# Two dense projections of a decoder block (w_o and w_xq) turned into streamed Strassen products, with the weight sums re-timed

## The chip, the cores and the metric

One core of one Trainium2 chip. The metric is the device time of the whole kernel in microseconds (us); the median of three runs before the change is 1949.75 us (1947.55 to 1952.03). Engines in the text: PE (TensorE, matrix products), DVE (VectorE), ACT (ScalarE), POOL (GpSimd), SP (SyncE, which issues nearly all the transfers between HBM and SBUF). Each engine works through its own queue in order, and so does SP with the transfers it issues.

## The reference, cut to what matters

The block has batch 1, 1024 tokens, width 1024 and one layer, all in float32: two mixers side by side (an SSD scan and a gated linear attention), their gated merge, an output projection `w_o` with a residual add, cross-attention to 256 memory tokens, and a SwiGLU feed-forward of inner width 2816.

```python
def hybrid_mixer(...):
    ...
    merged = jax.nn.sigmoid(g_ssd) * (y_ssd @ w_up_ssd) + jax.nn.sigmoid(g_gla) * (y_gla @ w_up_gla)
    return merged @ w_o

def mem_cross_attention(n, m, w_xq, w_xkv, w_xo):
    q = (n @ w_xq).reshape(Bsz, S, XATTN_HEADS, XATTN_HEAD_DIM)
    ...
    p = jax.nn.softmax(s, axis=-1).astype(v.dtype)
    o = jnp.einsum('bhsm,bmhd->bshd', p, v).reshape(Bsz, S, D_MODEL)
    return o @ w_xo

h = h + hybrid_mixer(rmsnorm(h, norm_mix), w_in, ...)
h = h + mem_cross_attention(rmsnorm(h, norm_xattn), rmsnorm(mem, norm_mem), w_xq, w_xkv, w_xo)
h = h + swiglu(rmsnorm(h, norm_ffn), w_ffn_in, w_ffn_out)
return rmsnorm(h, norm_final)
```

So `w_up_ssd`, `w_up_gla`, `w_o`, `w_xq` and `w_xo` are five products of 1024x1024 by 1024x1024, in this order, with the attention between the fourth and the fifth.

## The kernel before, in words

**Arithmetic.** Activations lie transposed (features on the 128 partitions, tokens along the row, in two halves of 512). A float32 product is made of three products of a shorter float type: each operand is split into a high part (ACT copies it, L227) and a low part (DVE subtracts, `split`, L226 to L228), and PE multiplies high by high, high by low and low by high into one PSUM bank. All matmuls are issued by one helper (L51), all DVE and POOL operations by another (L73), so groups of the trace are told apart by their tiles.

**Stages in order.** Input projection (Strassen), SSD, GLA, the products `w_up_ssd` (called dense 0), `w_up_gla` (1), `w_o` (2), `w_xq` (3), attention, `w_xo` (4), then the feed-forward: gate and up products as Strassen units, and the down product as a streamed Strassen.

**dense (L1236 to L1253)** is the classical product: 8 output blocks of 128 features by 2 halves of tokens, and for each 8 input blocks by 3 products, hence 16 x 24 = 384 matmuls of 128x512. Its weights come through `Left` (L1190 to L1219): one 1 MB load (`raw`, in a slot called "aux") brings 256 columns, and each 128 of them are split into a ring of two tiles `wd` two blocks ahead of their use. One `Left` serves all five products, so that the loads of one run on into the next. `residual` (L1357) adds the old residual to what `w_o` gives, stores the sum (`h1_d`), scales it and splits it into the operand of `w_xq` (`put_xq`), and adds up its squares (`s1`).

**presum (L1297 to L1318)** makes sums and differences of quarters of `w_ffn_out` for the streamed down product and keeps them in `down_d` in HBM. It works in 11 chunks on a single tile `pre`: one 1 MB load, four POOL operations of 128x512, four stores of 256 KB; the next load waits for the four stores. It runs beside dense 0 to 3 as a generator that is advanced in turns of the main loop (`run`, with a rate for each side job).

**The order of the work** on each engine is set by a scheduler that simulates a timeline of the program; `ahead()` gives operations a higher priority and `pinned` keeps them in program order. `either` gives an elementwise operation to POOL or to DVE, whichever an estimate expects to be done first (L85). Big tiles live in slots: 14 of "op", 4 of "aux", 4 of "m".

**Attention (L1412 to L1486)** has eight half heads in a software pipeline of scores, transposes and values. Keys and values come with `load_kv` (L1385). The loads of the first gate and up units of the feed-forward are issued during dense 4 (blocks 12 and 14).

## Time and profile before

| what | value |
|---|---|
| median of three runs | 1949.75 us (1947.55, 1949.75, 1952.03) |
| span of the profiled execution | 1949.0 us; the page gives no other time for it |
| PE busy | 1916.2 us, 98% of the span, 9776 matmuls and transposes |
| DVE, ACT, POOL busy | 1298.5 us (67%), 845.8 us (43%), 557.8 us (29%) |
| dense 0 to 3, from the trace | about 800 to 1156 us after the start |
| attention with what follows it, and dense 4 | 1156.5 to 1220 us, and 1220 to 1297 us |

The page is a table of one execution: the busy time of each engine, the costliest groups of instructions, and what ended the idle time ahead of them. The trace itself gives rows with a start, a duration, the engine, the line, the operation, its output and inputs, and in brackets how long the engine had been idle and which event ended that. A span is taken from the first to the last recorded work. SPq is the issuing side of SP.

### The profile page before, as it was taken

What the parts mean: (1) busy time and instruction counts of PE and PEld (TensorE: products, weight loads), DVE (VectorE), ACT (ScalarE), POOL (GpSimd) and SP (SyncE); (2) the same over time, 40 slices, a digit from 0 to 9 for tenths busy, and PEclk for the clock granted to TensorE, in tenths of its full rate; (3) what the DMA queues carried; (4) which work ended last, traced back from release to release, by engine and by line L of the source; (5) the groups of instructions that cost most, each with busy time, mean ns of one, the idle gap of its engine ahead of it and who ended that gap; (6) DMA issues with size and microseconds to landing.
All of it is one profiled execution on the core that took longest, in us unless ns stands there. A gap on an engine that the chain in (4) does not pass through costs nothing.

```text
span 1949.0 us, 26264 instructions
## 1 busy us (share of the span) xinstructions
PE 1916.2 (98%) x9776; PEld 1615.6 (83%) x9776; DVE 1298.5 (67%) x1873; ACT 845.8 (43%) x1485; POOL 557.8 (29%) x428
## 2 busy tenths in 40 slices
PE   7999999999999999999999999999999999999998
PEld 7998787888878888788887888888888888888888
DVE  7766879877776764655534237677777777766566
ACT  7534564655553444643223235444333333345243
POOL 0012334345543231022433000006445544320002
PEclk9999999999999999999999999999999999999999
DMA  9423383446553653997675201442233224177463
GB/s 341 144 93 101 130 307 107 152 161 186 174 173 123 198 167 124 348 346 270 226 269 164 82 22 44 140 141 82 90 126 110 82 100 144 42 271 239 157 224 126
DMA packets 237875, 317.98 MB, mean 163 GB/s; under 512 B 16538, under 2 KB 156036, under 8 KB 237748
## 3 DMA queue, kind: packets, MB, share of 16 engines
q1 hardware_dynamic: 236020, 310.01, 47.4%
q10 hardware_dynamic: 1728, 6.29, 0.8%
q8 instruction: 77, 1.26, 0.3%
q14 instruction: 50, 0.41, 0.1%
HBM read 215.27 MB, written 100.99 MB: 162 GB/s over the span
## 4 chain that ended last, share of the span: by engine, by line
PE 43%; DMA 3%; POOL 2%; DVE 1%; issue 1%; ACT 1%; POOLq 0%; SPq 0%; DVEq 0%; ACTq 0%
PE acc L51 38%; PE bank L51 4%; DMA pre<-in_w_ffn_out_dram 1%; POOL pre L73 1%; DMA down_d<-pre 1%; PE bank L55 1%; POOL ssum L73 0%; DVE hl L73 0%; POOL sa L73 0%; DMA h_d<-ga 0%; DMA ga<-vm_d 0%; DVE wd L73 0%; ACT wd L227 0%; ACT sq L493 0%; DVE phl L73 0%
## 5 line engine op out<-in xcount | busy, mean ns | idle before, releaser
L51 PE MATMUL acc<-hl,wd 128*128 128x512 f32 x1920 | 440.4, 390 | 3.6 <-DVE wd L73 2.0
L51 PEld LDWEIGHTS acc<-hl,wd 128*128 128x128 f32 x1920 | 359.6, 188 | 80.7 <-DVE wd L73 3.3
L73 DVE TENSOR_TENSOR wlo<-raw,whi 128x512 fp32r<-128x512 f32 x272 | 236.4, 875 | 103.6 <-ACT whi L227 103.5
L227 ACT ACTIVATE whi<-raw 128x512 fp32r<-128x512 f32 x272 | 169.5, 629 | 247.6 <-PE acc L51 201.0
L73 DVE TENSOR_TENSOR o<-acc,o 128x512 f32<-128x512 f32 (+1 forms) x256 | 172.6, 676 | 108.8 <-PE acc L51 95.4
L51 PE MATMUL acc<-fs 128*128 128x512 f32 (+1 forms) x792 | 155.7, 356 | 0.1
L51 PEld LDWEIGHTS acc<-fs 128*128 128x128 f32 x792 | 130.7, 189 | 20.8 <-issue 0.5
L73 DVE TENSOR_TENSOR fs<-fr,fs 128x1024 fp32r<-128x1024 f32 (+1 forms) x84 | 98.9, 1217 | 36.5 <-ACT fs L227 36.4
L227 ACT ACTIVATE fs<-fr 128x1024 fp32r<-128x1024 f32 (+1 forms) x84 | 79.2, 982 | 95.9 <-PE acc L51 31.2
L73 POOL TENSOR_TENSOR raw<-raw,sa 128x512 f32<-128x512 f32 x44 | 57.1, 1297 | 207.8 <-DVE wlo L73 207.8
L73 POOL TENSOR_TENSOR sa<-raw 128x512 f32<-128x512 f32 x43 | 69.6, 1619 | 107.0 <-DMA raw<-in_w_in_dram 78.9
L227 ACT ACTIVATE whi<-sa 128x512 fp32r<-128x512 f32 x96 | 59.6, 626 | 93.7 <-PE acc L51 92.3
L73 DVE TENSOR_TENSOR wlo<-sa,whi 128x512 fp32r<-128x512 f32 x96 | 80.9, 843 | 13.7 <-ACT whi L227 12.7
L73 DVE TENSOR_TENSOR wd<-raw,wd 128x1024 fp32r<-128x1024 f32 x40 | 52.8, 1323 | 47.6 <-ACT wd L227 47.2
L73 POOL TENSOR_TENSOR rstd<-rstd,mhalf 128x4 f32<-128x4 f32 (+1 forms) x7 | 8.7, 1246 | 257.0 <-DVE rstd L73 257.0
L227 ACT ACTIVATE wd<-raw 128x1024 fp32r<-128x1024 f32 x40 | 42.2, 1057 | 90.4 <-PE acc L51 89.8
L51 PE MATMUL acc<-T4h,whi 128*128 128x512 f32 x192 | 76.3, 397 | 2.4 <-DVE o L73 2.4
L51 PE MATMUL acc<-B22h,wlo 128*128 128x512 f32 x192 | 75.7, 394 | 1.5 <-DVE wlo L73 1.5
L51 PE MATMUL acc<-T1h,whi 128*128 128x512 f32 x192 | 76.3, 397 | 0.0
L51 PE MATMUL acc<-T2h,whi 128*128 128x512 f32 x192 | 75.9, 395 | 0.0
L51 PE MATMUL acc<-T3h,whi 128*128 128x512 f32 x192 | 75.9, 395 | 0.0
L51 PE MATMUL acc<-B22h,whi 128*128 128x512 f32 x192 | 75.7, 394 | 0.0
(399 smaller groups left out, 4698.6 us busy)
## 6 DMA issues: line engine op xcount, KB each, us to landing
raw<-in_w_in_dram SPq DMA_DIRECT2D x26, 1024.0 KB, 5.9
raw<-in_w_ffn_in_dram SPq DMA_DIRECT2D x22, 1024.0 KB, 6.5
act_d<-o SPq DMA_DIRECT2D x77, 256.0 KB, 2.1
fr<-act_d SPq DMA_DIRECT2D x35, 512.0 KB, 7.9
pre<-in_w_ffn_out_dram SPq DMA_DIRECT2D x11, 1024.0 KB, 10.0
fr<-down_d SPq DMA_DIRECT2D x20, 512.0 KB, 3.9
down_d<-pre SPq DMA_DIRECT2D x33, 256.0 KB, 3.1
h_d<-ga SPq DMA_DIRECT2D x32, 256.0 KB, 3.1
```

The source lines that it names most:

```text
L51: return s.e.matmul(o, x, y, **kw)
L55: return s.e.transpose(o, x, i)
L73: return f(*a, **kw)
L227: ACT.activation(hi, src, AF.Copy)
```

## The change

`w_o` and `w_xq` leave `dense` and become objects of a new class `Wide`. Each cuts the 1024x1024 weight and the operand into quarters and makes seven products of quarters (Strassen-Winograd: `B11`, `T1`, `B22`, `T2`, `B21`, `T3`, `T4`) in 14 steps of 24 matmuls. Four of the seven weight quarters are sums (`wos_d`, `xqs_d`); these are made by `presum`, whose first eight chunks are now `w_o` and `w_xq` and run beside dense 0 and 1, while its eleven chunks of `w_ffn_out` come later ("late"), three turns at each of the ten steps of the attention's pipeline and two at each of the 16 blocks of `w_xo`.

In a step, `prep` combines two quarters of the operand where needed (DVE, `rq`, in place), splits two blocks of the weights and two of the operand into a pair of tiles `ws`, and PE multiplies into four banks; `evac` empties them after the seven products' second step. Three products start in fresh banks; the others add to what the banks hold. For `w_o`, `evac` adds into tiles `wk` that were filled with the old residual; for `w_xq`, the first three are copied by ACT, the next three added by DVE, and the last is split straight into the attention's operand. `post_wo` stores a finished block, scales it into the operand of `w_xq` and adds up its squares. `post_yg` and `put_xq` no longer split, since `prep` does. The loads of the weight quarters, of the old residual and of keys and values are `pinned`. `w_xo` gets a `Left` of its own, first filled at step 12 of `w_xq`.

```diff
--- before.py
+++ after.py
+    wos_d = dram("wos_d", 2 * D, HALF)
+    xqs_d = dram("xqs_d", 2 * D, HALF)
...
+    class Wide:
+        SEQ = ("B11", "T1", "B22", "T2", "B21", "T3", "T4")
+        LEFT = {"B11": (0, 0), "B21": (0, 1), "T1": 0, "B22": 3, "T2": 1, "T3": 2, "T4": (1, 1)}
+        COMB = {"T1": ((0, 0), (0, 1), (0, 0)), "T2": ((0, 0), (1, 1), (0, 0)), "T3": ((0, 1), (1, 1), (0, 1)),
+                "T4": ((1, 0), (1, 0), (0, 0))}
+        RIGHT = {"B11": (0, 0), "B22": (1, 1), "B21": (1, 0), "T1": (0, 0), "T2": (0, 0), "T3": (0, 1), "T4": (1, 0)}
+        OUT = {"B11": (0, 0), "T1": (1, 1), "B22": (0, 1), "T2": (0, 1), "B21": (0, 0), "T3": (1, 1), "T4": (1, 0)}
+        def __init__(s, W, sums_d, post, keys, side, base=None, scale=1.0, two=None):
+            s.W, s.sums_d, s.post, s.keys, s.side, s.base, s.scale = W, sums_d, post, keys, side, base, scale
+            s.two = two or (lambda ap: DVE)
+            s.q, s.raw, s.ops, s.keep, s.chain = {}, [], [], {}, None
+        def quad(s, i, j):
+            if (i, j) not in s.q:
+                s.q[i, j] = slot("op", (P, 4, HALF), name="rq")
+            return s.q[i, j]
+        def load(s, n):
+            while len(s.raw) < min(n, 7):
+                src = s.LEFT[s.SEQ[len(s.raw)]]
+                if isinstance(src, tuple):
+                    i, j = src
+                    w = s.W[half(j), half(i)]
+                else:
+                    w = s.sums_d[half(src), :]
+                r = slot(s.keys[len(s.raw)], (P, 4, HALF), name="wr")
+                pinned(SP.dma_start(r, w.rearrange("(k p) c -> p k c", p=P)))
+                s.raw.append(r)
+        def home(s, i, j):
+            if (i, j) not in s.keep:
+                k = s.keep[i, j] = slot(s.side[len(s.keep)], (P, 4, HALF), name="wk")
+                if s.base is not None:
+                    pinned(SP.dma_start(k, s.base[half(i), half(j)].rearrange("(u p) c -> p u c", p=P)))
+            return s.keep[i, j]
+        def prep(s, n):
+            while len(s.ops) < min(n, 14):
+                m, kp = divmod(len(s.ops), 2)
+                s.load(m + 1)
+                name, c = s.SEQ[m], slice(2 * kp, 2 * kp + 2)
+                x = [slot("op", (P, 2, 2, HALF), F32R, name="ws") for _ in range(2)]
+                with ahead():
+                    if name in s.COMB:
+                        o, a, b = (s.quad(*ij)[:, c] for ij in s.COMB[name])
+                        sub(s.two(o), o, a, b)
+                    split(s.raw[m][:, c], x[0][:, 0], x[0][:, 1])
+                    split(s.quad(*s.RIGHT[name])[:, c], x[1][:, 0], x[1][:, 1])
+                s.ops.append(x)
+        def evac(s, name, u, p):
+            i, j = s.OUT[name]
+            o = p if name == "T4" and s.base is None else s.home(i, j)[:, u]
+            first = name in ("B11", "T1", "B22")
+            with ahead():
+                if s.base is not None:
+                    DVE.scalar_tensor_tensor(o, p, s.scale, o, ALU.mult, ALU.add)
+                elif first:
+                    ACT.activation(o, p, AF.Copy)
+                elif name != "T4":
+                    add(DVE, o, p, o)
+                if not first:
+                    s.post(i, j, u, o)
+        def steps(s):
+            x = 0
+            for m, name in enumerate(s.SEQ):
+                if name in ("B11", "T1", "B21"):
+                    banks = [(acc if name == "B11" else bank)() for _ in range(4)]
+                    if name == "B11":
+                        s.chain = banks
+                elif name in ("T2", "T3", "T4"):
+                    banks = s.chain
+                fresh = name in ("B11", "T1", "B21")
+                if s.base is not None:
+                    for z in s.SEQ[m:m + 2]:
+                        s.home(*s.OUT[z])
+                for kp in range(2):
+                    s.load(m + 3)
+                    s.prep(x + 3)
+                    w, b = s.ops[x]
+                    for u in range(4):
+                        for k in range(2):
+                            for n, (a, c) in enumerate(((0, 0), (0, 1), (1, 0))):
+                                PE.matmul(banks[u], w[:, a, k, u * P:(u + 1) * P], b[:, c, k],
+                                          start=fresh and kp + k + n == 0, stop=kp + k == 2 and n == 2,
+                                          skip_group_check=True)
+                    x += 1
+                    if kp:
+                        for u in range(4):
+                            s.evac(name, u, banks[u])
+                    yield
...
-    left = Left((t["w_up_ssd"], t["w_up_gla"], t["w_o"], t["w_xq"], t["w_xo"]))
+    left = Left((t["w_up_ssd"], t["w_up_gla"]))
...
-    s1 = Stats(rp)
-    def presum():
-        r = slot("m", (P, 2, D), name="pre")
-        for k in range(KP):
-            SP.dma_start(r, t["w_ffn_out"][256 * k:256 * k + 256, :].rearrange("(j p) c -> p j c", p=P))
+    s1 = Stats(rp, "ga", 6)
+    wides = (("w_o", wos_d), ("w_xq", xqs_d), )
+    def presum(part, key):
+        todo = [(t[w].rearrange("(j k p) c -> k p j c", j=2, p=P)[k], d, 4, k) for w, d in wides for k in range(4)]
+        todo += [(t["w_ffn_out"][256 * k:256 * k + 256, :].rearrange("(j p) c -> p j c", p=P), down_d, KP, k)
+                 for k in range(KP)]
+        r = slot(key, (P, 2, D), name="pre")
+        for src, dst, kn, k in todo[part]:
+            SP.dma_start(r, src)
...
-            put = lambda n, ap: SP.dma_start(down_d[(n * KP + k) * P:(n * KP + k + 1) * P, :], ap)
+            put = lambda n, ap: SP.dma_start(dst[(n * kn + k) * P:(n * kn + k + 1) * P, :], ap)
...
-        add(either(g), g, g, y)
-        into(i_wo, o, j, g)
+        q = wo.quad(o // 4, j)[:, o % 4]
+        add(either(g), q, g, y)
+    def post_wo(i, j, u, q):
+        o = 4 * i + u
+        SP.dma_start(h1_d[o * P:(o + 1) * P, half(j)], q)
+        put_xq(o, j, q, col("norm_xattn", o))
+        s1.take(j, q)
+    wo = Wide(t["w_o"], wos_d, post_wo, ("aux",) * 7, ("m", "m", "m", "aux"), xT_d, 0.5)
+    def wide_side(x, n):
+        for _ in range(n):
+            yield
+        x.load(2)
+        yield
+        x.prep(1)
+        yield
+        x.prep(2)
+        yield
...
+    xq = Wide(t["w_xq"], xqs_d, lambda i, j, u, p: into(i_q, 4 * i + u, j, p), ("aux", "m", "aux") * 3, ("m", "aux", "aux"))
     def put_xq(o, j, q, g):
-        x = hl(i_xq, o)
-        h, l = x[:, 0, half(j)], x[:, 1, half(j)]
-        ACT.activation(h, q, AF.Copy, scale=g)
-        DVE.scalar_tensor_tensor(l, q, g, h, ALU.mult, ALU.subtract)
+        ACT.activation(xq.quad(o // 4, j)[:, o % 4], q, AF.Copy, scale=g)
...
-    early = presum()
-    run(dense(0, i_ys, post_ys, lambda o, j: gate(gs_d, o, j)), (fetch_gated(yg_d, sr_d, i_yg), 1.0), (waiting(early, 12), 1.0))
-    run(dense(1, i_yg, post_yg, lambda o, j: (gate(gg_d, o, j), quad(ysg_d, o * P, 0, j))), (early, 1.1))
-    run(dense(2, i_wo, residual(h1_d, s1, "norm_xattn", put_xq, 0.5), quad_of(xT_d)), (early, 1.1))
+    early = presum(slice(0, 8), "m")
+    run(dense(0, i_ys, post_ys, lambda o, j: gate(gs_d, o, j)), (fetch_gated(yg_d, sr_d, i_yg), 1.0), (waiting(early, 2), 1.2))
+    run(dense(1, i_yg, post_yg, lambda o, j: (gate(gg_d, o, j), quad(ysg_d, o * P, 0, j))), (early, 1.5),
+        (wide_side(wo, 11), 1.0))
+    drain(early)
+    run(wo.steps())
...
+    def fetch_kv(h):
+        es = [rp.tile([P, 2, 256], F32, name="ga", tag="ga") for _ in range(2)]
+        pinned(SP.dma_start(es[0], kT_d[h * 256:(h + 1) * 256, :].rearrange("(i p) m -> p i m", p=P)))
+        pinned(SP.dma_start(es[1], vm_d[:, h * 256:(h + 1) * 256].rearrange("(i p) c -> p i c", p=P)))
+        return es
+    def split_kv(es, pin=lambda x: x):
+        h_ = slot("op" if kv else "m", (P, 2, 4, 256), F32R, name="kvhl")
+        for i in range(2):
+            pin(ACT.activation(h_[:, 0, 2 * i:2 * i + 2], es[i], AF.Copy))
+            pin(sub(DVE, h_[:, 1, 2 * i:2 * i + 2], es[i], h_[:, 0, 2 * i:2 * i + 2]))
+        kv.append(h_)
     def load_kv(h):
-        es = [rp.tile([P, 2, 256], F32, name="ga", tag="ga") for _ in range(2)]
-        h_ = slot("m" if h < 3 else "op", (P, 2, 4, 256), F32R, name="kvhl")
-        SP.dma_start(es[0], kT_d[h * 256:(h + 1) * 256, :].rearrange("(i p) m -> p i m", p=P))
-        SP.dma_start(es[1], vm_d[:, h * 256:(h + 1) * 256].rearrange("(i p) c -> p i c", p=P))
-        for i in range(2):
-            split(es[i], h_[:, 0, 2 * i:2 * i + 2], h_[:, 1, 2 * i:2 * i + 2])
-        kv.append(h_)
+        split_kv(fetch_kv(h))
...
-    run(dense(3, i_xq, lambda o, j, p, g: into(i_q, o, j, p)), (xq_side(), 1.0), (early, 1.0))
-    drain(early)
-    load_kv(0)
+    def kv_side():
+        for _ in range(2):
+            yield
+        es = fetch_kv(0)
+        for _ in range(9):
+            yield
+        split_kv(es, pinned)
+        yield
+    left_xo = Left((t["w_xo"],))
+    def next_left():
+        left_xo.upto(2)
+        yield
+    run(xq.steps(), (xq_side(), 1.0), (kv_side(), 1.0), (waiting(next_left(), 12), 1.0))
...
+    late = presum(slice(8, None), "op")
...
+        for _ in range(3):
+            next(late, None)
...
-    for n, _ in enumerate(dense(4, i_xo, residual(h2_d, u_xo_stats, "norm_ffn", put_xo), quad_of(h1_d), js=(1, 0))):
+    for n, _ in enumerate(dense(0, i_xo, residual(h2_d, u_xo_stats, "norm_ffn", put_xo), quad_of(h1_d), js=(1, 0), left=left_xo)):
+        for _ in range(2):
+            next(late, None)
```

On SP the order of the transfers changes at three places that the prediction speaks of. The first is the passage from `w_o` to `w_xq`. Before, the weights of `w_xq` are loaded among the loads of the old residual (`xT_d`), the chunks of `w_ffn_out` and the first stores of `h1_d` (shown as `h_d`):

```order
L1201 DMA raw<-in_w_o_dram 128x8x256
L1184 DMA ga<-xT_d 128x512
L1201 DMA raw<-in_w_xq_dram 128x8x256
L1302 DMA pre<-in_w_ffn_out_dram 128x2x1024
L1360 DMA h_d<-ga 128x512 x2
```

With the change:

```order
L1464 DMA h_d<-wk 128x512 x4
L1230 DMA wk<-xT_d 128x4x512
L1464 DMA h_d<-wk 128x512 x8
L1223 DMA wr<-in_w_xq_dram 128x4x512
L1223 DMA wr<-xqs_d 128x4x512 x3
L1511 DMA ga<-kT_d 128x2x256
```

The first load of `w_xq` has moved from the middle of `w_o` to behind the last of the 16 stores of its results.

The second place is the end of `w_up_gla`, where the first weights of `w_o` are loaded now, after the next to last chunk of the sums and before the last:

```order
L1411 DMA xqs_d<-pre 128x512 x3
L1223 DMA wr<-in_w_o_dram 128x4x512
L1407 DMA pre<-in_w_xq_dram 128x2x1024
L1411 DMA xqs_d<-sa 128x512
L1223 DMA wr<-wos_d 128x4x512
L1411 DMA xqs_d<-pre 128x512 x3
L1230 DMA wk<-xT_d 128x4x512 x2
```

Before, weights of `w_o` stood there one by one between the chunks; now the first two loads of `w_o` stand on both sides of the eighth chunk's load.

The third place is the end of `w_xo`, where the first up unit of the feed-forward gets its weights. Before, only residual blocks (`ga`, `h_d`) surround that load:

```order
L1564 DMA ga<-in_norm_final_dram 128x512
L1360 DMA h_d<-ga 128x512
L1184 DMA ga<-h_d 128x512
L293 DMA raw<-in_w_ffn_in_dram 128x8x256
L1360 DMA h_d<-ga 128x512
```

With the change:

```order
L1407 DMA pre<-in_w_ffn_out_dram 128x2x1024
L1713 DMA ga<-in_norm_final_dram 128x512
L1483 DMA h_d<-ga 128x512
L1411 DMA down_d<-sa 128x512
L1713 DMA ga<-in_norm_final_dram 128x512
L1411 DMA down_d<-pre 128x512 x3
L1483 DMA h_d<-ga 128x512
L1186 DMA ga<-h_d 128x512
L295 DMA raw<-in_w_ffn_in_dram 128x8x256
L1483 DMA h_d<-ga 128x512
```

The load now stands behind the last of the eleven late chunks, its load and its four stores.

4 lines of the change are left out of this document (2 added, 2 removed).

## The prediction

> **What bounds the kernel now.** I read the page's busy times first. In this fence and the later ones, rows are word for word.
>
> ```profile
> span 1949.0 us, 26264 instructions
> PE 1916.2 (98%) x9776; PEld 1615.6 (83%) x9776; DVE 1298.5 (67%) x1873; ACT 845.8 (43%) x1485; POOL 557.8 (29%) x428
> ```
>
> PE is busy for all but 32.8 us, so time is won by taking matmuls away and lost wherever something makes PE wait. Next I read the engines' busy time by stage (window, its length, then PE, PEld, DVE, ACT and POOL with counts, granted clock, share of the DMA engines, GB/s). The windows are dense 1, 2 and 3, attention, what follows it up to dense 4, and dense 4:
>
> ```profile
> 889.60:976.80 87.20, 87.20 (x386) 72.21 (x385) 48.51 (x54) 23.31 (x33) 35.61 (x24) 1.00 0.73 251
> 976.80:1068.00 91.20, 89.13 (x390) 72.55 (x389) 39.27 (x43) 28.11 (x41) 33.22 (x25) 1.00 0.66 219
> 1068.00:1156.50 88.50, 88.35 (x398) 73.07 (x397) 24.56 (x31) 20.50 (x30) 4.85 (x5) 1.00 0.20 63
> 1156.50:1198.40 41.90, 41.51 (x294) 37.90 (x293) 35.49 (x97) 29.71 (x85) 0.00 (x0) 1.00 0.08 26
> 1198.40:1220.20 21.80, 21.80 (x106) 18.19 (x105) 10.39 (x21) 8.47 (x18) 0.00 (x0) 1.00 0.15 49
> 1220.20:1297.00 76.80, 76.80 (x340) 63.62 (x339) 48.53 (x71) 35.53 (x57) 0.00 (x0) 1.00 0.42 141
> ```
>
> PE is the bound in each. DVE has 51.9 us free in dense 2 and 63.9 in dense 3, the two stages that change; POOL is empty from the attention to the end of dense 4. Last, PE's own timeline, runs of like matmuls with the wait ahead of each run in brackets:
>
> ```profile
> 804.50 185.71 PE L51 MATMUL acc<-hl,wd 128*128 128x512 f32 x818 [0.43 <-DVE wd L73]
> ...
> 1031.84 0.73 PE L51 MATMUL acc<-hl,wd 128*128 128x512 f32 x2 [0.38 <-ACT wd L227]
> 1033.34 21.60 PE L51 MATMUL acc<-hl,wd 128*128 128x512 f32 x94 [0.76 <-DVE wd L73]
> 1056.60 17.97 PE L51 MATMUL acc<-hl,wd 128*128 128x512 f32 x78 [0.78 <-DVE wd L73]
> 1074.73 9.36 PE L51 MATMUL acc<-hl,wd 128*128 128x512 f32 x40 [0.15 <-DVE hl L73]
> ```
>
> The first row gives the price of a matmul: 818 in 185.71 us, 0.227 us each. So 24 of them, a step of the new projections, take 5.45 us, and a new projection of 14 steps 76.2 us. The other rows are all of PE's waits in and just behind dense 2 that I count: 0.38 + 0.76 + 0.78 + 0.15 = 2.07 us.
>
> **The change part by part.**
>
> *a. Fewer matmuls.* Each projection goes from 384 to 336, so 96 x 0.227 = **-21.8 us**. All lie on PE's path.
>
> *b. Dense 2's waits* come from its `wd` ring, which the new projection doesn't have: **-2.1 us** (between -2.1 and 0, if the new splits come as late).
>
> *c. The start of w_xq.* Its first weight load stands on SP behind all 16 stores of `w_o`, and the last of these waits for DVE's last evacuation of `T4`, which waits for PE. Nothing else is left for PE to do, so what was hidden inside dense 2 becomes a wait. Prices:
>
> ```profile
> 1255.83 0.38 SPq L293 DMA_DIRECT2D raw<-in_w_ffn_in_dram  x1
> 1261.04 0.69 DVE L73 TENSOR_TENSOR sa<-raw 128x512 f32<-128x512 f32 x1 [1.21 <-DMA raw<-in_w_ffn_in_dram]
> ...
> L73 DVE SCALAR_TENSOR_TENSOR ga<-acc,ga 128x512 f32<-128x512 f32 x16 | 10.9, 683 | 12.2 <-PE acc L51 12.2
> L227 ACT ACTIVATE wd<-raw 128x1024 fp32r<-128x1024 f32 x17 | 17.9, 1055 | 39.3 <-PE acc L51 38.7 <-ACT ssum L490 0.6
> L73 DVE TENSOR_TENSOR fs<-fr,fs 128x1024 fp32r<-128x1024 f32 (+1 forms) x84 | 98.9, 1217 | 36.5 <-ACT fs L227 36.4
> pre<-in_w_ffn_out_dram SPq DMA_DIRECT2D x11, 1024.0 KB, 10.0
> ```
>
> From PE's end: 0.7 for the evacuation, two issues of about 0.4, then 5.2 for a 1 MB load to reach its reader (1261.04 - 1255.83): 6.7. ACT's two high parts (1.06 each, weight and operand) bring the first matmul to 8.8. DVE's low parts, 1.22 each behind ACT's, bring the full flow to about 10.2, by which time four matmuls (0.9) are done: 9.3 us lost. A pause of PE also shows at the granted clock (matmul in this fence: a pause of 1.74 us ahead of it; windows of 2 us, the last but two columns the clock):
>
> ```profile
> 53.74 0.39 PE L51 MATMUL bank<-wlo,mh 128*128 128x256 f32 x1 [1.74 <-DVE wlo L73]
> 52.00:54.00 2.00, 0.26 (x3) 0.26 (x3) 2.00 (x4) 0.56 (x1) 0.00 (x0) 1.00 1.09 360
> 54.00:56.00 2.00, 2.00 (x14) 1.78 (x14) 2.00 (x4) 0.65 (x1) 0.00 (x0) 0.77 1.05 402
> 56.00:58.00 2.00, 2.00 (x11) 2.00 (x11) 2.00 (x5) 0.00 (x0) 0.00 (x0) 0.50 0.27 94
> 58.00:60.00 2.00, 2.00 (x17) 2.00 (x16) 2.00 (x4) 1.91 (x4) 0.00 (x0) 0.87 0.05 11
> ```
>
> After it the clock was at 0.77, 0.50 and 0.87 for 2 us each, (0.23 + 0.50 + 0.13) x 2 = 1.7 us lost. I take the same here. **c = +11.0 us.** Lower end +7: operand split early, so one ACT copy less, no clock loss. Upper end +16: the three loads issued right behind share the engines, and the first takes the 10.0 us that the last row but the windows shows for a 1 MB load in company.
>
> *d. The end of dense 1.* The first split of `w_o` stands on DVE ahead of the split of the last `wd` of dense 1, and waits for a load behind the seventh chunk of sums. The side job that orders it starts after 11 of 16 blocks, 889.6 + 11 x 5.45 = 949.6; load and four splits end near 960, and PE needs that `wd` two blocks before 976.8, at 965.9. About 6 us of cover, if the chunks keep up: **+2 us** (0 to 6: the first sums of eight need 8 x 16.2 us at the worst four-step mean of part g, which would take up the whole cover), nearer to nothing.
>
> *e. Inside the projections.* For `w_o` DVE has 28 evacuations x 0.683 = 19.1, 28 splits x 1.217 = 34.1, 8 combinations, not shown in this form, at the split's price 9.7, and up to 14 additions of squares at some 0.69 = 9.7: 72.6 of 76.2 us. ACT's 28 splits are 28 x 1.055 = 29.5. The cover is thin (3.6 us), yet holds: **0** (0 to 2). For `w_xq` three evacuations of seven go to ACT, and DVE has room.
>
> *f. Attention.* POOL's sums now run beside it; DVE has 6.4 us free there and few operations that read SBUF twice: **+1 us** (0 to 4).
>
> *g. The start of the feed-forward.* The first up unit's load now stands behind all eleven late chunks. A chunk can't start before the former's stores have landed. The cadence, by the starts of the first POOL operation of four chunks in a row and a fifth:
>
> ```profile
> 956.87 2.16 POOL L73 TENSOR_TENSOR sa<-pre 128x512 f32<-128x512 f32 x1 [8.56 <-issue]
> 971.21 1.29 POOL L73 TENSOR_TENSOR sa<-pre 128x512 f32<-128x512 f32 x1 [7.53 <-DMA pre<-in_w_ffn_out_dram]
> 984.92 1.29 POOL L73 TENSOR_TENSOR sa<-pre 128x512 f32<-128x512 f32 x1 [7.76 <-DMA pre<-in_w_ffn_out_dram]
> 1005.81 1.28 POOL L73 TENSOR_TENSOR sa<-pre 128x512 f32<-128x512 f32 x1 [14.29 <-DMA h_d<-ga]
> 1021.77 1.28 POOL L73 TENSOR_TENSOR sa<-pre 128x512 f32<-128x512 f32 x1 [7.53 <-DMA pre<-in_w_ffn_out_dram]
> ```
>
> Steps of 14.3, 13.7, 20.9 and 16.0 us; 20.9 is a store of the residual that held up SP. The first late load stands behind those of step 12 of `w_xq`, two to three steps before the attention: 15 us, an estimate. From there to the latest issue are 15 + 41.9 + 21.8 + 76.8 - 5.2 = 150.3 us; the last chunk doesn't count its landing, 13.7 - 5.2 (load) - 4 x 1.29 = 3.3 us. So eleven chunks fit up to (150.3 + 3.3) / 11 = 14.0 us each. The two quick steps average 14.0 and would cost nothing; I take 14.25, since SP has other transfers between the chunks: **+3 us** (0 to 22, at 16.0 us a chunk).
>
> Sum: -21.8 - 2.1 + 11.0 + 2 + 0 + 1 + 3 = -6.9 us. Span 1949.0 - 6.9 = 1942.1, and with the 0.75 by which the median lies above the span **1943 us**.
>
> *A rule against the change.* In dense 1 a POOL pair of 2.99 us and DVE's low split overlap:
>
> ```profile
> 912.15 2.99 POOL L73 TENSOR_TENSOR pre<-pre 128x512 f32<-128x512 f32 x2
> 913.92 2.31 DVE L73 TENSOR_TENSOR wd<-raw,wd 128x1024 fp32r<-128x1024 f32 x1
> ```
>
> The split took 2.31 instead of 1.22, 1.09 more, less than one POOL operation (1.5). The Trainium skill ("SBUF — State Buffer", section "SBUF: two separate sides") says that a DVE operation with two SBUF inputs and a GpSimd operation that reads SBUF lock each other out for a whole instruction. This trace agrees in kind; a full lock is rival 2.
>
> **The rivals.**
>
> *1. The price of the new start is at its lower end and all else stays covered:* -21.8 - 2.1 + 7 = -16.9, so **1933 us**. For it: PE has no other wait in attention and dense 4 today. Against: the stores are ahead of the load on SP, and the clock did fall after a shorter pause.
>
> *2. DVE becomes the bound by the lock.* With 8 of the additions of squares on POOL (1.4 each, between the 1.29 and the 1.5 of POOL's rows above), `w_o` has 72.6 - 5.5 + 11.2 = 78.3 us of DVE: +2.1. In dense 4 some 22 POOL operations of 1.5 lock out its 48.5 us: 81.5 against 76.8, +4.7. Together **1950 us** (1943 + 6.8). For it: thin cover in `w_o`. Against: the evacuations read PSUM, and the split lost only 1.09.
>
> *3. Slower: the late sums don't keep up.* PE stands at the first up unit until the eleventh chunk's stores are issued. Each us of cadence above 14.0 costs 11. At 15.5 us this is +16.5 instead of +3, **1957 us**; from 14.9 on (3 + 6.9 = 9.9 over 11) nothing of the gain is left. For it: the four steps above average 16.2. Against: the longest of them was set by a store of the residual, and the chain starts with POOL empty.
>
> **How the numbers follow.** My forecast has 0.46, rival 1 0.16, rival 2 0.12, rival 3 0.26. A measurement of this kernel can't tell less than 0.2%, 3.9 us, from no change. Faster (below 1945.9): rival 1 and nearly all of the forecast, 0.61. Within: rival 2, the forecast's rest and a third of rival 3, 0.22. Slower: the rest of rival 3, 0.17. The forecast's own range is 1937 to 1950; 1933 to 1957 leaves out the far part of rival 3 and the luckiest of rival 1.
>
> **What would show it.** Right: the matmuls of the two projections number 672; PE has one pause of 8 to 10 us ahead of `w_xq`'s first product, released by ACT or DVE on `ws`, with two or three windows of a lower clock behind it; no wait over 1 us inside `w_o`; the last late chunk's stores end within 5 us of the end of dense 4. Wrong: no such pause (c too dear), many short waits of PE on `ws` (e), or PE waiting at the feed-forward's start for a load by `w_ffn_in` (g).

## The result and the profile after

The changed kernel is slower: 1969.86 us median of four runs (1967.21 to 1972.94) against 1948.65 us for the kernel before beside it (1946.68 to 1952.03), a ratio of 1.0117 (95% interval 1.0102 to 1.0132). The forecast was 1943 us, with 1933 to 1957 as its wider range.

From the page of the changed kernel: its span, and busy times of the engines.

```profile
span 1968.2 us, 26272 instructions
PE 1907.3 (97%) x9680; PEld 1604.2 (82%) x9680; DVE 1373.1 (70%) x1927; ACT 880.7 (45%) x1521; POOL 593.9 (30%) x454
```

The 96 matmuls are gone (9776 to 9680), but PE's busy time fell only by 8.9 us, not by 21.8: matmuls at a slow clock count as busy for longer, and the mean granted clock is 0.989 instead of 0.998. And PE stands idle for 60.9 us of the span instead of 32.8. PE's waits from 780 to 1340 us of the changed kernel (what was waited for: us in total, times, the longest):

```profile
PE acc L51 <- ACT ws L229: 9.0, 1, 9.0
PE acc L51 <- DVE wd L73: 7.2, 2, 6.8
PE acc L51 <- ACT whi L229: 5.9, 3, 4.6
PE acc L51 <- ACT wd L229: 4.7, 3, 3.2
PE bank L51 <- DVE phl L73: 2.2, 2, 1.3
...
PE bank L55 <- DVE pe L73: 1.3, 2, 0.8
```

PE's own timeline tells where they lie (start, length, run of like matmuls, in brackets the wait ahead of it):

```profile
969.36 1.79 PE L51 MATMUL acc<-hl,wd 128*128 128x512 f32 x4 [3.21 <-ACT wd L229]
977.99 12.79 PE L51 MATMUL acc<-hl,wd 128*128 128x512 f32 x44 [6.83 <-DVE wd L73]
990.62 11.04 PE L51 MATMUL acc<-ws 128*128 128x512 f32 x48
...
1045.02 21.92 PE L51 MATMUL acc<-ws 128*128 128x512 f32 x96
1075.97 8.04 PE L51 MATMUL acc<-ws 128*128 128x512 f32 x28 [9.03 <-ACT ws L229]
...
1155.51 7.12 PE L51 MATMUL acc<-kvhl,hl 128*128 128x256 f32 x58
...
1304.75 0.39 PE L51 MATMUL acc<-B11h,whi 128*128 128x512 f32 x1
...
1312.27 0.79 PE L51 MATMUL acc<-B11h,whi 128*128 128x512 f32 x1 [4.63 <-ACT whi L229]
```

Here `acc` and `bank` are banks of PSUM, `hl` and `whi` high (and low) parts of operands and weights. The rows without a wait are borders of stages: `w_o` begins at 990.62, its last run ends at 1066.94, the attention begins at 1155.51, the feed-forward at 1304.75. Against the borders before (976.80, 1068.00, 1156.50, 1297.02) the 19.2 us of the two spans' difference divide so:

| stretch | before | after | difference | forecast |
|---|---|---|---|---|
| up to the end of dense 1 | 976.8 | 990.6 | +13.8 | +2 (d) |
| `w_o` | 91.2 | 76.3 | -14.9 | -13.0 (half of a; b, e) |
| the pause and `w_xq` | 88.5 | 88.6 | +0.1 | +0.1 (half of a; c, e) |
| attention to the end of dense 4 | 140.5 | 149.2 | +8.7 | +1 (f) |
| feed-forward to the end | 652.0 | 663.5 | +11.5 | +3 (g) |

The two stretches of the new projections came out as forecast. The three around them, which take no matmul from PE, cost 34.0 us. Each has its own trace.

**End of dense 1.** The granted clock there (windows, length, then PE, PEld, DVE, ACT, POOL busy with counts, clock, share of the DMA engines, GB/s):

```profile
970.00:973.00 3.00, 1.16 (x3) 0.34 (x2) 3.00 (x3) 0.00 (x0) 3.00 (x2) 0.50 0.64 121
973.00:978.00 5.00, 0.01 (x1) 0.01 (x1) 5.00 (x4) 0.00 (x0) 2.72 (x2) 0.50 0.94 347
978.00:980.00 2.00, 2.00 (x5) 1.61 (x6) 2.00 (x3) 0.00 (x0) 0.00 (x0) 0.50 0.23 11
980.00:982.00 2.00, 2.00 (x7) 1.52 (x5) 2.00 (x3) 0.00 (x0) 0.00 (x0) 0.50 0.88 321
982.00:984.00 2.00, 2.00 (x7) 1.59 (x6) 0.69 (x2) 0.00 (x0) 0.00 (x0) 0.66 1.04 406
```

So 10.0 us of waiting, and 3.8 us more while PE comes back at half its clock. What it waited for stands on three engines' timelines:

```profile
953.58 1.30 POOL L73 TENSOR_TENSOR sa<-pre 128x512 f32<-128x512 f32 x1 [8.16 <-DMA pre<-in_w_xq_dram]
956.27 2.81 SPq L1411 DMA_DIRECT2D xqs_d<-pre  x3
959.14 0.43 SPq L1223 DMA_DIRECT2D wr<-in_w_o_dram  x1
965.56 1.22 DVE L73 TENSOR_TENSOR ws<-wr,ws 128x1024 fp32r<-128x1024 f32 x1 [14.27 <-ACT ws L229]
...
968.43 2.30 DVE L73 TENSOR_TENSOR ws<-wr,ws 128x1024 fp32r<-128x1024 f32 x1
970.65 1.75 DVE L73 TENSOR_TENSOR rq<-wlo,ga 128x512 f32<-128x512 f32 x1
972.32 2.28 DVE L73 TENSOR_TENSOR ws<-rq,ws 128x1024 fp32r<-128x1024 f32 x1
974.52 2.28 DVE L73 TENSOR_TENSOR rq<-rq 128x1024 f32<-128x1024 f32 x1
976.72 1.21 DVE L73 TENSOR_TENSOR wd<-raw,wd 128x1024 fp32r<-128x1024 f32 x1
```

The first sums of the chunks start at 821.5, 859.3, 886.4 and 909.6 us, 38, 27 and 23 apart, and only then every 14 to 16 us. So the seventh chunk's stores leave SP at 956 to 959, and the load of `w_o` comes behind them, 9.5 us later than the prediction put it (949.6). DVE idles 14.3 us until ACT has copied that load. The split of dense 1's last `wd` is queued behind what DVE then does for `w_o` and for the last blocks of dense 1, and four of these operations run while POOL works on the eighth chunk (967.82 to 975.72): they take 2.30, 1.75, 2.28 and 2.28 us, where the same forms take 1.22, 0.69, 1.22 and 1.22 elsewhere in this trace, 4.3 us more in all. The `wd` split ends 18.8 us behind the issue of the load; the prediction had some 10 between them.

**Attention.** DVE's groups from the attention to dense 4, first of the kernel before, then of the changed one (count, busy us, mean ns):

```profile
L73 DVE TENSOR_SCALAR pe<-pe,sm 128x256 f32<-128x256 f32 x32 | 9.9, 348 | 0.2
L73 DVE SCALAR_TENSOR_TENSOR mx<-mx,xsc 128x2 f32<-128x2 f32 x16 | 2.4, 150 | 0.0
```

```profile
L73 DVE TENSOR_SCALAR pe<-pe,sm 128x256 f32<-128x256 f32 x32 | 18.6, 622 | 0.4
L73 DVE SCALAR_TENSOR_TENSOR mx<-mx,xsc 128x2 f32<-128x2 f32 x16 | 5.3, 334 | 0.1
```

The scaling of the exponentials (`pe`) takes 622 ns instead of 348, that of the maxima (`mx`) 334 instead of 150: 11.6 us more of DVE, while operations that read PSUM keep their 0.68 us. DVE has 43.0 busy us in the first 50.9 there, and PE waits for `pe` and for the split of the transposed exponentials (`phl`). Over the whole 149.2 us PE is idle for 5.6 us (0.4 before) and busy for 143.7 (140.1 before).

**Feed-forward.** The sums of the eleven late chunks start between 1150.70 and 1295.07, 14.4 us apart on average, and the first up unit's load leaves SP just after dense 4 has ended. The chain of events that ended last, from the eleventh chunk's last store on (start, length, what):

```profile
1300.25 0.32 SPq L1411
...
1300.61 4.23 DMA h_d<-ga
...
1305.26 6.30 DMA raw<-in_w_ffn_in_dram
```

So behind the chunk's last store (L1411) comes the store of a residual block (`h_d`), 4.2 us until it has landed; a load on SP waits for that, and the up unit's load stands behind it.

### The profile page after: what moved, and what is told of

It reads as the page before. It is cut to its first block, busy times and chain, and to the rows that moved or that the text cites. A ratio compares the mean times of both kernels' runs of the same rounds, so it can differ in the third digit from the quotient of the medians.

```text
span 1968.2 us, 26272 instructions
## 1 busy us (share of the span) xinstructions
PE 1907.3 (97%) x9680; PEld 1604.2 (82%) x9680; DVE 1373.1 (70%) x1927; ACT 880.7 (45%) x1521; POOL 593.9 (30%) x454
## 5 line engine op out<-in xcount | busy, mean ns | idle before, releaser
L51 PE MATMUL acc<-hl,wd 128*128 128x512 f32 x1152 | 267.5, 393 | 12.0 <-DVE wd L73 7.2
L51 PEld LDWEIGHTS acc<-hl,wd 128*128 128x128 f32 x1152 | 217.4, 190 | 60.4 <-DVE wd L73 8.9
L73 POOL TENSOR_TENSOR sa<-pre 128x512 f32<-128x512 f32 x19 | 26.9, 1414 | 263.6 <-DMA pre<-in_w_o_dram 104.7
L51 PE MATMUL acc<-ws 128*128 128x512 f32 x384 | 90.3, 394 | 9.0 <-ACT ws L229 9.0
L51 PEld LDWEIGHTS acc<-ws 128*128 128x128 f32 x384 | 73.0, 191 | 24.7 <-ACT ws L229 9.5
L51 PE MATMUL acc<-B11h,whi 128*128 128x512 f32 x192 | 76.2, 397 | 4.6 <-ACT whi L229 4.6
L51 PE MATMUL acc<-T4h,whi 128*128 128x512 f32 x192 | 76.2, 397 | 2.0 <-DVE o L73 2.0
L51 PE MATMUL acc<-T1h,wlo 128*128 128x512 f32 x192 | 75.8, 395 | 1.0 <-DVE wlo L73 1.0
```

The source lines that it names most:

```text
L51: return s.e.matmul(o, x, y, **kw)
L73: return f(*a, **kw)
```

## The experiments

Twelve runs. Each is compared with the kernel before on the same chip; the changed kernel stands at 1.0117 on that scale, and 0.001 is 1.9 us.

**Is it the first load of `w_o`?** The load moves five blocks forward in dense 1, nothing else.

```diff
-        for _ in range(n):
+        for _ in range(n - 5):
+            yield
+        x.load(1)
+        for _ in range(5):
             yield
         x.load(2)
```

> Changed kernel, with one edit: the first weight load of w_o is issued five blocks earlier in dense 1, so that it stands on SP ahead of the last store of the sixth chunk of sums instead of behind the seventh chunk. Theory (the 13.8 us lost at the end of dense 1 come from that load's place behind the sums, which came late): the two waits of 3.2 and 6.8 us of PE there shrink to under 2 us together, the clock stays at 1.00, and the time falls by 10 to 13 us, to about 1958. Rival (DVE and ACT have too much queued ahead of the last wd split there, whenever the load comes): PE still waits 6 us or more and the time stays within 4 us of 1970.

Ratio 1.0101 (1.0086 to 1.0116): some 3 us better, with intervals that overlap. Three other profiles of the first runs, whose edits don't touch this place, also have `w_o` starting 3 us ahead of 990.62 (at 987.0 to 987.7). Both waits at the end of dense 1 are gone, but PE's timeline shows two new ones inside `w_o`:

```profile
974.41 8.32 PE L51 MATMUL acc<-ws 128*128 128x512 f32 x36
...
1001.59 0.79 PE L51 MATMUL acc<-ws 128*128 128x512 f32 x1 [5.26 <-ACT ws L229]
1005.85 3.53 PE L51 MATMUL acc<-ws 128*128 128x512 f32 x8 [3.46 <-DVE ws L73]
```

`w_o` starts at 974.41 instead of 990.62, and waits 8.7 us at its third product, whose weights (sums again) are loaded behind the eighth chunk's stores and two 1 MB loads of the residual (issued by SP at 984.67, landed at 999.5). The load's place was the cause of the wait where it was seen, as the theory said; the gain it promised did not come, since the next load in the same queue was late too. The time stayed within 4 us, as the rival said, for another reason than the rival's.

**What do POOL's sums cost beside the attention?** The POOL operations of the late chunks are left out, all their transfers stay.

```diff
-            add(POOL, s1_, a(1, 0), a(1, 1))
-            put(0, s1_)
+            if kn == 4:
+                add(POOL, s1_, a(1, 0), a(1, 1))
+            put(0, s1_ if kn == 4 else a(0, 0))
...
```

> Changed kernel, but the four POOL operations of each of the eleven late chunks are left out (the chunks are loaded and stored as they are, so down_d and with it the output of the feed-forward hold wrong sums); all transfers stay. Theory (beside attention POOL's sums hold up DVE's operations, and at the feed-forward's start the chain of chunks is too long): attention up to dense 4 falls from 71.2 us to 64 to 66 as without sums, the wait ahead of the first up unit goes since chunks take 9 us instead of 14.4, and the time falls by 17 to 20 us to about 1951. Rival (the transfers of the sums and the key and value loads behind them are what delays attention): attention stays above 69 us, only the feed-forward's start is mended, about 1959.

Ratio 1.0044 (1.0029 to 1.0059), 14 us better. DVE's group in the attention is back at its old length:

```profile
L73 DVE TENSOR_SCALAR pe<-pe,sm 128x256 f32<-128x256 f32 x32 | 9.8, 349 | 0.3
```

Attention to the end of dense 4 takes 143.7 us (1152.26 to 1295.94) instead of 149.2, and the wait ahead of the first up unit is gone. So 5.5 of the 8.7 us go with POOL's operations; 3.2 stay without them. The edit leaves both the chunks' transfers and the new order of the program in place, so it doesn't tell which of these the 3.2 belong to. The theory was right on both places, with 17 to 20 us a little too high.

**Is it the up unit's load?** It is asked for at block 9 of dense 4.

```diff
-        if n == 14:
+        if n == 9:
             gu[0][1].load()
```

> Changed kernel, with one edit: the first up unit's weight load is asked for at block 9 of dense 4 instead of 14, which puts it on SP ahead of the tenth late chunk's stores. Theory (the feed-forward's start waits for this load alone): PE's 4.6 us wait there and the slow clock behind it go, with the three short waits on the second loads mostly, and the time falls by 8 to 11 us to about 1960. Rival (ACT and DVE are late there because of the sums and operand work, the load is only the last of several): PE still waits 3 us or more in the first 30 us of the feed-forward, and the time falls by under 4 us.

Ratio 1.0107 (1.0089 to 1.0126): no gain beyond the intervals. The load left SP at 1271.21, well ahead of dense 4's end (1303.57), yet PE waits 0.93 and 0.92 us for late residual blocks (`DVE ga`) and then 4.33 us for weights:

```profile
1307.38 0.50 PE L51 MATMUL acc<-B11h,whi 128*128 128x512 f32 x1 [0.93 <-DVE ga L73]
...
1319.45 0.79 PE L51 MATMUL acc<-T1h,whi 128*128 128x512 f32 x1 [4.33 <-ACT whi L229]
```

What was late in its place shows on DVE's timeline:

```profile
1292.08 0.69 DVE L73 TENSOR_TENSOR raw<-raw 128x512 f32<-128x512 f32 x1
1298.25 0.91 DVE L73 TENSOR_TENSOR sa<-sa,raw 128x512 f32<-128x512 f32 x1 [5.48 <-POOL pre L73]
```

The up unit's second sum of weights stands 5.5 us until POOL has worked on the eleventh chunk: both take their small tiles (`sa`) from the same pair (L308 and L1410 of the changed kernel). Residual evacuations and splits queue behind it on DVE. The rival held: the chain of sums holds this place by more than the one load.

**Is the pause ahead of `w_xq` the load behind the stores?** Its first two loads and its first step move to steps 10 to 13 of `w_o`.

```diff
-    run(wo.steps())
+    def xq_first():
+        for _ in range(10):
+            yield
+        xq.load(2)
+        yield
+        yield
+        xq.prep(1)
+        yield
+
+    run(wo.steps(), (xq_first(), 1.0))
```

> Changed kernel, with one edit: the first two weight loads of w_xq are issued, and its first step split, from steps 10 to 13 of w_o, so that the loads stand on SP ahead of the last eight stores of w_o. Theory (the 9.0 us pause ahead of w_xq is the load behind the stores): the pause shrinks to under 2 us, the clock stays up, and the time falls by 8 to 10 us to about 1961. Rival (the operand quarter or DVE's queue of last evacuations would hold w_xq up as long anyway): a pause of 5 us or more stays and the time falls by under 4 us.

Ratio 1.0045 (1.0030 to 1.0060), 14 us better. PE's timeline has no wait left between the first matmul of `w_o` (987.53) and the attention (1141.70): 154.2 us, of which 672 x 0.227 = 152.5 are the matmuls. The changed kernel takes 164.9 us for the same, so 10.7 us of the gain lie here; 3.1 lie ahead of `w_o`, which the edit doesn't touch. Nothing came in this wait's place. The later runs whose expectation names this edit keep it.

**Sums of `w_xq` beside `w_o`.** The run before, the earlier load of `w_o`, and the four chunks of `w_xq` moved from dense 1 to beside `w_o`:

```diff
-    early = presum(slice(0, 8), "m")
+    early = presum(slice(0, 4), "m")
...
+    mid = presum(slice(4, 8), "m")
+    run(wo.steps(), (mid, 2.0), (xq_first(), 1.0))
```

> Changed kernel with the earlier load of w_o and the earlier loads and first step of w_xq, as in the two runs before, and the four chunks of w_xq's sums moved from dense 1 to beside w_o, so that no sum stands on SP between the loads of w_o's first products. Theory (at the end of dense 1 every load of w_o queues behind the chain of sums, not the first alone): PE's waits at the passage from dense 1 to w_o and in w_o's first four steps fall from about 10 us to under 3 us in all, clock 1.00 there; with w_xq's pause gone too the time is 1940 to 1944, a little under the kernel before. Rival (DVE has no room in w_o: the POOL sums beside it lock its operations and PE waits on splits all along w_o): w_o takes 84 us or more instead of 76 and the time stays at 1950 or above.

Ratio 1.0045 (1.0030 to 1.0060), the same as the run before. Dense 1 ends at 974.09 without a wait, but in `w_o` one wait of 6.45 us for `wk` appears:

```profile
1047.69 19.79 PE L51 MATMUL acc<-ws 128*128 128x512 f32 x76 [6.45 <-DVE wk L73]
```

The fourth residual tile's load now stands on SP behind the moved chunks' stores, the evacuation needs that tile, and the next product needs the bank. The theory missed. The rival's numbers came true (`w_o` takes 86 us, the time is above 1950), but its reason only in small part: DVE's splits of weights take 1.39 us on average there instead of 1.22, and PE waits 0.74 and 0.35 us for splits (`ws`).

**Sums of `w_ffn_out` beside `w_xq`.** Five of the late chunks go there, the other six start with the eighth of attention's ten steps:

```diff
-    run(xq.steps(), ...)
+    mid = presum(slice(8, 13), "m")
+    run(xq.steps(), ..., (mid, 1.8), ...)
+    drain(mid)
...
-        for _ in range(3):
+        for _ in range(3 if n > 6 else 0):
             next(late, None)
```

> The kernel of the run before, and the chunks of w_ffn_out moved: five beside w_xq, none beside the first seven of attention's ten steps, six from there through dense 4. Theory (POOL's sums cost the attention 5 to 7 us, and the eleven chunks in a chain end too late for the feed-forward): attention up to dense 4 takes 64 to 66 us instead of 71, the 11.5 us at the feed-forward's start shrink to under 4, together 13 us less than the run before, about 1929. Rival (the sums beside w_xq cost there what they cost the attention, and six chunks from the attention's end still end too late): w_xq takes 4 us or more longer, the first up load still comes last, and the time falls by under 6 us.

Ratio 1.0114 (1.0098 to 1.0129), worse by 13 us. PE waits 8.35 us inside `w_xq` (for `wk`, an evacuation by ACT) and 7.73 us at the start of the attention, and the feed-forward's start still has 4.4 us of waits. The attention with dense 4 is shorter, 145.8 us instead of 150.1, but that is the smaller part. The next run asks for the up unit's load earlier in this kernel:

> The kernel of the run before, and the first up unit's load asked for at block 9 of dense 4 instead of 14. Theory (with a shorter chain no later load is behind sums): 0 to 3 us less than the run before, the feed-forward starts without a wait over 1 us. Rival (the next units' loads or DVE's late residual blocks wait in its place, as when this load alone was moved): no change within 2 us.

Ratio 1.0073 (1.0056 to 1.0090), 7 us better than the run before it, where the theory had 0 to 3: behind a shorter chain the moved load does help. Its pauses in and behind `w_xq` are the same (8.43 and 8.32 us).

**Is it SP's queue, or the sums themselves?** In the changed kernel POOL, not SP, issues the loads and stores of the sums; nothing else is edited.

```diff
-            SP.dma_start(r, src)
+            nc.gpsimd.dma_start(r, src)
...
-            put = lambda n, ap: SP.dma_start(dst[...], ap)
+            put = lambda n, ap: nc.gpsimd.dma_start(dst[...], ap)
```

> Changed kernel, with one edit: all loads and stores of the weight sums are issued by POOL, beside the operations they belong to, instead of by SP; order of the sums, their operations and all else as in the changed kernel. Theory (SP's queue in order is what makes others wait: w_o's loads at the end of dense 1 and the up unit's load stand behind stores that wait for POOL): the 10 us of waits and 3.8 us of slow clock at the end of dense 1 fall to under 3 us, and the wait at the feed-forward's start falls from 6.9 to under 2 us; the pause ahead of w_xq (9.0) and the attention's (71 us) stay; time about 1969 - 11 - 9 = 1949. Rival (the bandwidth of the sums' transfers or POOL's operations themselves delay them): waits at the same places stay above 8 and 4 us, time above 1962.

Ratio 1.0171 (1.0121 to 1.0220): slower than the kernel before, and no better than the changed kernel, though the first half of the theory came true:

```profile
804.23 177.13 PE L51 MATMUL acc<-hl,wd 128*128 128x512 f32 x768 [4.03 <-ACT wd L229]
...
1317.88 1.84 PE L51 MATMUL bank<-ones,ssum 128*128 128x1 f32 x8 [5.91 <-DVE ssum L73]
```

Dense 0 and 1 run through to `w_o` (981.19) without a wait: with SP free of the sums, nothing there is late. But the chain also begins 27 us earlier (its first sum at 794.40 instead of 821.46), and the run doesn't separate the two. Against this gain stand 4.0 us at the start of dense 0, where the chain now begins, and 18 us in five waits at the feed-forward's start. There POOL's chain is still at work. Its late steps are 15.4 to 16.2 us for the first five, then 16.3 to 21.2, and the last load leaves only at 1323.04, behind an operation for the norm (`rstd`) in POOL's own queue:

```profile
1289.15 0.71 POOL L1407 DMA_DIRECT2D pre<-in_w_ffn_out_dram  x1 [4.53 <-DMA down_d<-pre]
...
1300.30 3.60 DVE L73 TENSOR_TENSOR wlo<-raw,whi 128x512 fp32r<-128x512 f32 x1 [12.34 <-ACT whi L229]
```

SP issues the up unit's load at 1289.80, 0.6 us behind a chunk's load, and ACT gets it at 1299.6, 9.8 us later instead of 5.2; then DVE's split takes 3.60 us instead of 0.69 beside POOL's operations. So the second half of the theory was wrong: at that place the chain hurts on any queue as long as it isn't over. The same with `w_xq`'s loads earlier:

> The kernel of the run before with w_xq's first loads and first step issued from steps 10 to 13 of w_o. Theory (causes on separate queues add up): the pause ahead of w_xq goes and nothing comes in its place, 9 to 12 us less than the run before, about 1938, under the kernel before by some 0.4%. Rival (a pause taken away comes back at the next load): within 4 us of the run before.

Ratio 1.0087 (1.0060 to 1.0115), 16 us better than the run before it: `w_xq`'s pause is gone again, with nothing in its place there. That is more than the 9 to 12 us of the theory, but far from its 1938 us, since the run before it was so much slower than expected. The two runs' times spread (1957 to 1968 and 1971 to 1989 us), more than those of the runs ahead of them.

**Spread the chain evenly.** On POOL's queue, 13 chunks from dense 0 through `w_o`, none in `w_xq` and most of the attention, six late:

```diff
-    early = presum(slice(0, 8), "m")
+    early = presum(slice(0, 13), "m")
...
+    run(wo.steps(), (early, 1.8), (xq_first(), 1.0))
+    drain(early)
...
-    late = presum(slice(8, None), "op")
+    late = presum(slice(13, None), "op")
```

> The kernel of the run before (sums issued by POOL, w_xq's loads earlier), and the chunks spread anew: the chain starts four turns into dense 0 and runs on through w_o with the first five chunks of w_ffn_out (13 in all), none beside w_xq and the first seven of attention's ten steps, the last six from there through dense 4. Theory (each loss has its own cause: SP's queue, POOL beside the attention, a chain that ends too late for the feed-forward): no wait over 1 us from dense 1 to w_xq, attention up to dense 4 64 to 66 us instead of 71, under 2 us of waits at the feed-forward's start; 1926 to 1934, 0.6 to 1.0% under the kernel before. Rival (POOL's sums beside w_o lock DVE, which has hardly 4 us free there, and the last six still end late): w_o takes 3 us or more longer and 6 us or more stay at the feed-forward's start; 1945 or above.

Ratio 1.0044 (1.0025 to 1.0064), with ten runs between 1944 and 1961 us. The feed-forward's start is nearly clean (1.1 us), but 3.3 us stay at dense 0, 5.0 us ahead of `w_xq` for `wk`, and 150.2 us for the attention and dense 4. The theory's number was not met. The rival's was (1945 or above), but not its reasons: `w_o` has no wait inside it. With fourteen:

> The kernel of the run before, with one chunk more beside w_o (14) and one fewer late (5). Theory: the fourteenth ends in w_xq, within 2 us of the run before; if the late chain was still too long there, it gains what was left of the waits at the feed-forward's start. Rival: the fourteenth chunk keeps a slot and POOL's queue too long, and w_xq pauses by 3 us or more for a slot or for the scales of the norm.

Ratio 1.0045 (1.0028 to 1.0062): the same time, with the waits in other places (2.15 and 2.58 us ahead of and in `w_xq`, 4.42 in dense 4). The theory's "within 2 us" held.

**Half of the change.** `w_xq` alone as a streamed product, `w_o` classical, so 15 chunks instead of 19, issued by SP, with only three of them late and `w_xq`'s first loads asked for earlier:

```diff
-    left = Left((t["w_up_ssd"], t["w_up_gla"]))
+    left = Left((t["w_up_ssd"], t["w_up_gla"], t["w_o"]))
...
-    wides = (("w_o", wos_d), ("w_xq", xqs_d), )
+    wides = (("w_xq", xqs_d), )
...
-    run(wo.steps())
+    run(dense(2, i_wo, residual(h1_d, s1, "norm_xattn", put_xq, 0.5), quad_of(xT_d)), (early, 1.8), (xq_first(), 1.0))
+    drain(early)
...
-    late = presum(slice(8, None), "op")
+    late = presum(slice(12, None), "op")
```

> Half of the change: w_xq alone is a streamed Strassen product, w_o stays the classical dense 2 with its split operand (48 matmuls saved instead of 96); so 15 chunks of sums instead of 19, all issued by SP: the four of w_xq first, then eight of w_ffn_out, beside dense 0 to 2, the last three from the eighth of attention's ten steps on; w_xq's first loads and first step are issued from block 10 of dense 2. Theory (the change loses because the chain of sums needs more time than there is beside work that can spare POOL, DVE and SP; with four chunks fewer it fits): no wait over 1 us ahead of or in w_xq, attention up to dense 4 64 to 67 us, under 2 us at the feed-forward's start; 48 x 0.227 = 10.9 us less than the kernel before less 2 to 4 us of small waits, ratio 0.995 to 0.997. Rival (what the new projection's splits, combinations and loads cost in DVE's and SP's time is lost however few the sums are): ratio 1.000 or above.

Ratio **0.9959** (0.9945 to 0.9973): 1938.55 us against 1946.28, 0.4% faster than the kernel before. PE's timeline and windows:

```profile
802.62 259.62 PE L51 MATMUL acc<-hl,wd 128*128 128x512 f32 x1144 [0.39 <-DVE wd L73]
```

```profile
976.80:1062.08 85.28, 85.28 (x377) 70.59 (x377) 37.33 (x43) 30.26 (x43) 22.71 (x16) 1.00 0.66 224
1062.08:1140.09 78.01, 78.01 (x353) 64.87 (x352) 59.03 (x70) 45.67 (x62) 2.00 (x2) 1.00 0.44 149
1140.09:1285.61 145.52, 141.51 (x737) 119.38 (x736) 96.24 (x185) 71.89 (x155) 15.28 (x12) 1.00 0.36 123
```

Dense 0 to 2 are one run of matmuls, `w_xq` has PE busy for all of its 78.0 us, the clock is 1.00 throughout. The attention and dense 4 cost 5.0 us more than before, with three chunks beside them. The rival is out: what a streamed product costs DVE and SP doesn't eat up its gain. The run differs from the changed kernel in several things at once (which projections, how many chunks, where they lie, when `w_xq`'s first loads are asked for), so it shows that a version of this kind pays, not which of the differences mattered.

## Why the prediction was wrong, point by point

**Right.** Matmuls removed and their price (a), with dense 2's waits (b): `w_o` takes 76.3 us, 76.2 was said. Part c: a pause of 9.0 us released by ACT on `ws`, and a clock of 0.50 and 0.77 for 2 us each behind it (rows below), 1.5 us: 10.5 together where 11.0 was said, and the run that moved the load confirmed the cause. Part e for `w_o`: no wait inside it, though with far more room than was said. DVE is busy for 54.0 of the 76.3 us, not 72.6: six of the 28 splits and four of the eight combinations came before `w_o`, and POOL took seven of the additions of squares. What came before `w_o` stood in part ahead of dense 1's last `wd`.

```profile
1067.00:1076.00 9.00, 0.03 (x1) 0.03 (x1) 2.36 (x3) 3.91 (x7) 1.85 (x2) 0.78 0.91 309
1076.00:1078.00 2.00, 2.00 (x5) 1.62 (x6) 2.00 (x3) 2.00 (x3) 0.00 (x0) 0.50 1.05 403
1078.00:1080.00 2.00, 2.00 (x9) 1.59 (x8) 2.00 (x3) 1.09 (x2) 0.00 (x0) 0.77 1.05 387
```

**Wrong, d: the end of dense 1, +13.8 instead of +2 (0 to 6).** The failing step is the cover of 6 us "if the chunks keep up", with 16.2 us a chunk for all eight. That cadence came from rows of late dense 1 and dense 2; the chain now starts in dense 0, where the first steps were 38, 27 and 23 us. The kernel before had chunks in dense 0 too, and its trace has their price, steps of 31 and 28 us:

```profile
833.98 1.28 POOL L73 TENSOR_TENSOR sa<-pre 128x512 f32<-128x512 f32 x1 [47.69 <-DMA pre<-in_w_ffn_out_dram]
...
865.21 1.60 POOL L73 TENSOR_TENSOR sa<-pre 128x512 f32<-128x512 f32 x1 [25.00 <-DMA pre<-in_w_ffn_out_dram]
...
892.95 1.29 POOL L73 TENSOR_TENSOR sa<-pre 128x512 f32<-128x512 f32 x1 [20.96 <-DMA pre<-in_w_ffn_out_dram]
```

So the right rows were at hand and the rate was carried over from another stage. Much of the slow start is the transfers themselves: with the sums on POOL's queue the steps in dense 0 are still 23 to 25 us, the DMA engines' share is 0.99 to 1.06 from 816 to 886, and a chunk's load takes 9.1 to 10.6 us until its reader starts, where the last two in dense 1 take 5.5. A second term was mis-sized: "load and four splits", some 10 us, became 18.8, of which 4.3 are operations of DVE that were slow beside POOL's; no run took POOL's operations away at this place. The upper bound of 6 was no bound at all, since it stopped where the cover ended, and the half clock behind a wait, priced in c, was not priced here.

**Wrong, f: the attention, +8.7 instead of +1 (0 to 4).** The step that failed is "few operations that read SBUF twice". DVE lost 2.9 us there on 16 operations that do (`mx`, two small inputs in SBUF, 150 to 334 ns), and 8.7 us on 32 that read one tensor from SBUF (`pe`, 348 to 622); without POOL's operations they were back at 155 and 349. The Trainium skill ("SBUF — State Buffer", section "SBUF: two separate sides") names two kinds of DVE operation in that lock, those with two SBUF inputs and those in a two-port mode. The prediction took up only the first. The second would fit `pe`: in the kernel before, a scaling of this kind (`yt`) took 346 ns at 128x256 and 752 at 128x1024, half as much per column as a subtraction of two tensors (683 at 128x512, 1217 at 128x1024); but the trace does not name the mode. As rival 2 the lock was looked for in `w_o` and dense 4, not here.

**Wrong in size, g: the feed-forward, +11.5 instead of +3 (0 to 22).** The mechanism, and its place as rival 3, were right, and the mean cadence of 14.4 us was close to the 14.25 taken. Three terms were mis-sized. The chain began 10.7 us ahead of the attention, not 15. The load was taken to follow the last chunk's stores at once: the last of these was out at 1300.57, only 1.0 us after the latest good time, but the residual block's store and load in between made it 5.7 (1305.26). And the price of being late was taken as the lateness alone: PE's four waits came to 6.9 us, and the slow clock behind them (0.50 to 0.53 from 1312 to 1318 and 0.50 from 1325 to 1328) to most of the rest.

**The rivals.** Rival 3 was priced at 1957 us from its own place alone; the measured time needed d and f beside it. That several places might lose together was left out of the range's upper end (1957). In sum, d, f and g came to 34.0 us where 6 were said. The signs named for being right all came, among them the pause ahead of `w_xq` and the last late chunk's stores near the end of dense 4; one sign of being wrong came too, PE waiting at the feed-forward's start. None looked at the end of dense 1 or at the attention, where 22.5 of the 34.0 us went.

**The common cause.** Single loads moved out of the way of the sums (first and third run) brought nothing clear of the intervals, since the next transfers waited for the same chain; with the sums off SP's queue, and begun earlier, the wait at dense 1 vanished, while the feed-forward's start, where the chain of chunks itself ended late, did not mend. Two limits fit all of this: SP's order, and the time that 19 chunks take one after the other on one tile. That the second is met with fifteen chunks is shown only together with the other differences of the last run. What the 3.2 us are that the attention loses without POOL's operations stays open.

## What to carry to other kernels

A side job that shares an in-order queue with the main work costs by its latest step: before pricing a load behind it, walk the whole chain from its new start, with rows of the stage it now starts in, and price the next load in the queue too, and the slow clock behind every pause. Count what an extra projection asks of the side engines (here four more chunks of 14 us) before counting what it saves on PE; half of such a change can pay where the whole does not. When moving one load brings nothing, look at what stands next in the same queue.

## What the runs showed of the hardware

- PE came back at a clock of 0.50 after pauses of 3.2, 6.8, 9.0 and 4.6 us, and stayed there or near it for 2 to 6 us; the 10.0 us of waits at the end of dense 1 cost 13.8. Three short waits in a row (0.46, 0.84 and 0.95 us between 1320 and 1325) were also followed by 0.50, from 1325 to 1328.
- Beside POOL's operations on SBUF, DVE's splits of 128x1024 took 2.28 to 2.30 us instead of 1.22 at the end of dense 1; in the attention a DVE operation with one SBUF tensor of 128x256 took 622 instead of 348 ns on average, in one place 2.54 us for two of them, while operations with a PSUM input kept 0.68 us. With POOL issuing the transfers too, a split of 128x512 once took 3.60 instead of 0.69.
- POOL issued its transfers in 0.55 to 0.78 us each (the first took 0.92). Its chain of chunks had steps of 25 to 23 us at first and 15.4 to 21.2 late, where SP's had 38 to 23 and 14.4 on average: quicker in dense 0, slower late.
- A chunk's 1 MB load on POOL's queue reached its reader in 9.1 to 10.6 us in dense 0, where the DMA engines' share was 0.99 to 1.06, and in 5.5 us for the last two in dense 1 (share 0.76 from 914 to 928).
